# Local window attention: q and k loaded in 512-row blocks, four consecutive rows to a partition

## The chip, the cores and the metric

The kernel runs on one core of one Trainium2 chip. The profile is one execution of the same program taken by the hardware profiler; its span is about 1.8 us shorter than the timed execution it belongs to.

## The reference

Attention inside windows of 64 tokens, with q, k, v of shape (4, 4096, 1536) in float32:

```python
q_w = q.reshape(B, nw, W, D)            # W = 64, nw = S // W; k_w, v_w likewise
logits = np.einsum('bnwd,bnud->bnwu', q_w, k_w) * D ** -0.5
logits = logits - logits.max(axis=-1, keepdims=True)
attn = np.exp(logits)
attn = attn / attn.sum(axis=-1, keepdims=True)
out = np.einsum('bnwu,bnud->bnwd', attn, v_w)
```

Each input and the output is 100.66 MB, so 402.65 MB have to cross HBM whatever the kernel does.

## The kernel before

One group is 128 tokens (two windows). For each of the 128 groups, three loads issued by POOL convert float32 to bf16, PE transposes q and k chunk by chunk, DVE copies the transposed chunks out of PSUM (the memory that PE writes) to SBUF, PE makes the logits, ACT takes the exponential of the two diagonal blocks, PE multiplies by v, ACT scales the result while copying it out of PSUM (the evacuation), and SP stores.

```python
for b in range(B):
    for g in range(n_groups):
        t0 = g * P
        q_nat = q_pool.tile([P, D], bf16)                       # q, k, v pools: 3 buffers each
        nc.gpsimd.dma_start(out=q_nat, in_=q[b, t0:t0 + P, :])
        # ... k_nat and v_nat likewise
        qkt = qkt_pool.tile([P, 2 * n_chunks, 128], bf16)
        for bank in range(3):
            tp = tp_psum.tile([P, 8, 128], bf16)
            # ... 8 PE transposes of q and k chunks into tp
            nc.vector.tensor_copy(out=qkt[:, bank * 8:(bank + 1) * 8, :], in_=tp)
        # ... 12 matmuls into lg
        attn = attn_pool.tile([P, P], bf16)                     # 3 buffers
        nc.gpsimd.memset(attn, 0.0)
        # ... exp of two 64x64 blocks into attn; row sums (matmul with ones); reciprocal
        for cc in range(3):
            # ... av = attn^T v, 512 columns
            nc.scalar.mul(out_sbuf[:, cc * 512:(cc + 1) * 512], av, recip)
        nc.sync.dma_start(out=out[b, t0:t0 + P, :], in_=out_sbuf)
```

The softmax here doesn't subtract the row's maximum and nothing guards it: scores larger than these inputs give would overflow.

Of the kernel before, what the change touches and what calls it, by code (L numbers as in the profile page):

```python
# [1 line left out]

# [5 lines left out]


@with_exitstack
def kernel(
    ctx: ExitStack,
    tc: tile.TileContext,
    q: bass.AP,
    k: bass.AP,
    v: bass.AP,
    out: bass.AP,
):
    nc = tc.nc  # L20
    fp32 = mybir.dt.float32
    bf16 = mybir.dt.bfloat16

    B, S, D = q.shape
    W = 64
    P = 128
    n_groups = S // P
    n_chunks = D // 128
    scale = float(D) ** -0.5

    EXP = mybir.ActivationFunctionType.Exp

    const_pool = ctx.enter_context(tc.tile_pool(name="const_pool", bufs=1))
    q_pool = ctx.enter_context(tc.tile_pool(name="q_pool", bufs=3))
    k_pool = ctx.enter_context(tc.tile_pool(name="k_pool", bufs=3))
    v_pool = ctx.enter_context(tc.tile_pool(name="v_pool", bufs=3))
    qkt_pool = ctx.enter_context(tc.tile_pool(name="qkt_pool", bufs=2))
    attn_pool = ctx.enter_context(tc.tile_pool(name="attn_pool", bufs=3))
    out_pool = ctx.enter_context(tc.tile_pool(name="out_pool", bufs=3))
    small_pool = ctx.enter_context(tc.tile_pool(name="small_pool", bufs=4))  # L40

    tp_psum = ctx.enter_context(tc.tile_pool(name="tp_psum", bufs=3, space=bass.MemoryType.PSUM))
    lg_psum = ctx.enter_context(tc.tile_pool(name="lg_psum", bufs=2, space=bass.MemoryType.PSUM))
    av_psum = ctx.enter_context(tc.tile_pool(name="av_psum", bufs=3, space=bass.MemoryType.PSUM))

    identity = const_pool.tile([128, 128], bf16)
    make_identity(nc, identity)
    ones_col = const_pool.tile([128, 1], bf16)
    nc.gpsimd.memset(ones_col, 1.0)

    for b in range(B):
        for g in range(n_groups):
            t0 = g * P

            q_nat = q_pool.tile([P, D], bf16)
            nc.gpsimd.dma_start(out=q_nat, in_=q[b, t0:t0 + P, :])  # L56
            k_nat = k_pool.tile([P, D], bf16)
            nc.gpsimd.dma_start(out=k_nat, in_=k[b, t0:t0 + P, :])  # L58
            v_nat = v_pool.tile([P, D], bf16)
            nc.gpsimd.dma_start(out=v_nat, in_=v[b, t0:t0 + P, :])  # L60

            qkt = qkt_pool.tile([P, 2 * n_chunks, 128], bf16)
            for bank in range(3):
                tp = tp_psum.tile([P, 8, 128], bf16)
                for j in range(8):
                    slot = bank * 8 + j
                    c, is_k = divmod(slot, 2)
                    src = k_nat if is_k else q_nat
                    nc.tensor.transpose(  # L69
                        tp[:, j, :], src[:, c * 128:(c + 1) * 128], identity  # L70
                    )
                nc.vector.tensor_copy(  # L72
                    out=qkt[:, bank * 8:(bank + 1) * 8, :], in_=tp
                )

            lg = lg_psum.tile([P, 136], fp32)
            for c in range(n_chunks):
                nc.tensor.matmul(  # L78
                    lg[:, 0:128],
                    lhsT=qkt[:, 2 * c + 1, :],  # L80
                    rhs=qkt[:, 2 * c, :],
                    start=(c == 0),
                    stop=(c == n_chunks - 1),
                )

            attn = attn_pool.tile([P, P], bf16)
            nc.gpsimd.memset(attn, 0.0)  # L87
            nc.scalar.activation(  # L88
                out=attn[0:W, 0:W], in_=lg[0:W, 0:W], func=EXP, scale=scale
            )  # L90
            nc.scalar.activation(  # L91
                out=attn[W:P, W:P], in_=lg[W:P, W:P], func=EXP, scale=scale
            )

            nc.tensor.matmul(  # L95
                lg[:, 128:129], lhsT=attn, rhs=ones_col, start=True, stop=True
            )
            recip = small_pool.tile([P, 1], fp32)
            nc.vector.reciprocal(out=recip, in_=lg[:, 128:129])  # L99

            out_sbuf = out_pool.tile([P, D], fp32)
            for cc in range(3):
                av = av_psum.tile([P, 512], fp32)
                nc.tensor.matmul(  # L104
                    av,
                    lhsT=attn,
                    rhs=v_nat[:, cc * 512:(cc + 1) * 512],
                    start=True,
                    stop=True,
                )  # L110
                nc.scalar.mul(out_sbuf[:, cc * 512:(cc + 1) * 512], av, recip)  # L111

            nc.sync.dma_start(out=out[b, t0:t0 + P, :], in_=out_sbuf)


# [1 line left out]
_INS = ['q', 'k', 'v']  # L117
_OUTS = [((4, 4096, 1536), 'float32')]


# [23 lines left out]
```

## Time and profile before

| | before |
|---|---|
| time, median of 13 runs | 974.66 us (973.48 to 976.4) |
| span of the profile | 971.7 us |
| HBM traffic over the span | 414 GB/s |
| the same between 200 and 800 us | 418.9 GB/s |
| from the last load's landing to the end | 8.2 us |

The third row is the page's own figure. The fourth and fifth are worked out from the trace's DMA packet records: every data packet is counted with its larger, float32 side (6144 bytes for one row), and its bytes are spread evenly over its recorded time. All rates called "steady rate" below are made in this way over 200 to 800 us.

Lines of the page of the kernel before: busy time by engine, the span in 40 slices (busy tenths), the DMA queues (packets, MB, share of 16 engines), groups of instructions (busy us, mean ns | idle before them, releaser), and DMA issues (KB each, us to landing).

```profile
span 971.7 us, 13347 instructions
PE 580.6 (60%) x5120; PEld 432.2 (44%) x5120; DVE 277.2 (29%) x512; ACT 292.8 (30%) x641; POOL 230.4 (24%) x519
...
DMA  9999999999999999999999999999999999999997
...
q0 software_dynamic: 55296, 151.02, 79.2%
q1 hardware_dynamic: 18432, 100.67, 26.2%
...
L69 PE MATMUL tp<-identity,q_nat 128*128 128x128 bf16 x1536 | 337.8, 273 | 214.0 <-DMA q_nat<-in_q_dram 214.0
...
L111 ACT ACTIVATE out_sbuf<-av,recip 128x512 f32<-128x512 f32 x384 | 235.8, 685 | 257.6 <-PE av L104 253.1
...
L72 DVE COPY qkt<-tp 128x1024 bf16<-128x1024 bf16 x384 | 255.8, 689 | 142.1 <-PE tp L69 132.3
...
out_dram<-out_sbuf SPq DMA_DIRECT2D x128, 768.0 KB, 7.8
q_nat<-in_q_dram POOLq DMA_DIRECT2D x128, 384.0 KB, 16.3
```

The DMA row is at 9 tenths in all slices but the last, while no compute engine is busy more than 60%. PE, the busiest of them, stands idle for q_nat 214.0 us. The DMA engines bound this kernel. Queue q0 carries the loads; 55296 packets are 49152 data packets (one row each) and 6144 completion packets of 4 bytes, 16 for each of 384 loads. GB/s counts the SBUF side, where a loaded row is bf16, so its value moves with the mix of loads and stores and is not the HBM rate.

### The profile page before, as it was taken

The page shows a single profiled execution, that of the slowest core. Times are in us where ns is not written, and L with a number is a line of the kernel's source. Part 1 is how long each engine was busy: PE and PEld are TensorE (multiplying, and loading weights), DVE is VectorE, ACT ScalarE, POOL GpSimd, SP SyncE. Part 2 cuts the span into 40 slices and gives each one's busy share as a digit, 9 for nine tenths or more (in the row PEclk, how much of TensorE's full clock was granted, in tenths as well). Part 3 has the DMA queues.
Part 4 walks back from the last instruction along what each step waited for, and adds up shares of the span by engine and source line. Part 5 has one row for each costly group of instructions (what it writes and reads, how often), then busy time and mean ns, then how long its engine had stood idle before and what let it go on. Part 6 is the DMA issues. An engine that isn't in the chain of part 4 may idle for free. (4 is left out here: it accounts for less than half of the span.)

```text
span 971.7 us, 13347 instructions
## 1 busy us (share of the span) xinstructions
PE 580.6 (60%) x5120; PEld 432.2 (44%) x5120; DVE 277.2 (29%) x512; ACT 292.8 (30%) x641; POOL 230.4 (24%) x519
## 2 busy tenths in 40 slices
PE   4665765656556566465565655675546656576564
PEld 3444544444444344344444444454434434354443
DVE  2222332223222232232222322223222322232222
ACT  2222322223223232232222322233223222232233
POOL 4222222222122222222222222222222222222220
PEclk9677667678677776776767767657787676766767
DMA  9999999999999999999999999999999999999997
GB/s 184 265 259 269 265 259 260 264 269 259 259 263 261 268 259 259 273 257 263 259 260 274 259 259 261 264 267 259 259 270 261 262 259 259 272 261 259 263 261 230
DMA packets 73791, 252.53 MB, mean 260 GB/s; under 512 B 8192, under 2 KB 8192, under 8 KB 73728
## 3 DMA queue, kind: packets, MB, share of 16 engines
q0 software_dynamic: 55296, 151.02, 79.2%
q1 hardware_dynamic: 18432, 100.67, 26.2%
q8 instruction: 40, 0.66, 0.2%
q14 instruction: 23, 0.19, 0.0%
HBM read 301.99 MB, written 100.66 MB: 414 GB/s over the span
## 5 line engine op out<-in xcount | busy, mean ns | idle before, releaser
L69 PE MATMUL tp<-identity,q_nat 128*128 128x128 bf16 x1536 | 337.8, 273 | 214.0 <-DMA q_nat<-in_q_dram 214.0
L69 PE MATMUL tp<-identity,k_nat 128*128 128x128 bf16 x1536 | 270.8, 277 | 169.7 <-DMA k_nat<-in_k_dram 169.7
L111 ACT ACTIVATE out_sbuf<-av,recip 128x512 f32<-128x512 f32 x384 | 235.8, 685 | 257.6 <-PE av L104 253.1
L69 PEld LDWEIGHTS <-k_nat 128*128 128x128 bf16 x1536 | 190.1, 129 | 253.7 <-DMA k_nat<-in_k_dram 196.8
L69 PEld LDWEIGHTS <-q_nat 128*128 128x128 bf16 x1536 | 192.5, 126 | 241.0 <-DMA q_nat<-in_q_dram 240.3
L72 DVE COPY qkt<-tp 128x1024 bf16<-128x1024 bf16 x384 | 255.8, 689 | 142.1 <-PE tp L69 132.3
L60 POOL DMA_DIRECT2D v_nat<-in_v_dram x128 | 67.7, 529 | 612.4 <-PE tp L69 582.2
L78 PE MATMUL lg<-qkt 128*128 128x128 bf16 x1536 | 178.5, 262 | 1.0 <-DVE qkt L72 0.8
L99 DVE RECIPROCAL recip<-lg 128x1 f32<-128x1 f32 x128 | 21.5, 168 | 546.3 <-PE lg L95 532.0
L104 PE MATMUL av<-v_nat,attn 128*128 128x512 bf16 x384 | 158.2, 541 | 0.0
L88 ACT ACTIVATE attn<-lg 64x64 bf16<-64x64 f32 x128 | 27.8, 217 | 403.2 <-PE lg L78 403.2
L78 PEld LDWEIGHTS <-qkt 128*128 128x128 bf16 x1536 | 134.3, 121 | 9.2 <-DVE qkt L72 9.2
L56 POOL DMA_DIRECT2D q_nat<-in_q_dram x128 | 67.7, 529 | 66.3 <-PE tp L69 60.6
L58 POOL DMA_DIRECT2D k_nat<-in_k_dram x128 | 68.3, 533 | 38.5 <-DMA v_nat<-in_v_dram 32.0
L104 PEld LDWEIGHTS <-attn 128*128 128x128 bf16 x384 | 37.3, 122 | 28.5 <-issue 23.5
L87 POOL MEMSET attn<- 128x128 bf16 x128 | 28.7, 224 | 0.0
L91 ACT ACTIVATE attn<-lg 64x64 bf16<-64x64 f32 x128 | 27.9, 218 | 1.5
L95 PE MATMUL lg<-ones_col,attn 128*128 128x1 bf16 x128 | 25.0, 196 | 0.7 <-ACT attn L91 0.7
L95 PEld LDWEIGHTS <-attn 128*128 128x128 bf16 x128 | 16.9, 132 | 0.8 <-issue 0.8
L88 ACT ACT_TABLE_LOAD x1 | 1.3, 1283 | 12.5 <-PE lg L78 12.5
masks.py:199 POOL TENSOR_SCALAR_AFFINE_SELECT identity<-identity 128x128 bf16<-128x128 bf16 x1 | 0.3, 304 | 0.1
masks.py:197 POOL MEMSET identity<- 128x128 bf16 x1 | 0.2, 204 | 0.3 <-POOLq L128 0.3
(5 smaller groups left out, 0.5 us busy)
## 6 DMA issues: line engine op xcount, KB each, us to landing
out_dram<-out_sbuf SPq DMA_DIRECT2D x128, 768.0 KB, 7.8
q_nat<-in_q_dram POOLq DMA_DIRECT2D x128, 384.0 KB, 16.3
k_nat<-in_k_dram POOLq DMA_DIRECT2D x128, 384.0 KB, 17.8
v_nat<-in_v_dram POOLq DMA_DIRECT2D x128, 384.0 KB, 15.9
```

What stands on the lines that cost most here:

```text
L56: nc.gpsimd.dma_start(out=q_nat, in_=q[b, t0:t0 + P, :])
L58: nc.gpsimd.dma_start(out=k_nat, in_=k[b, t0:t0 + P, :])
L60: nc.gpsimd.dma_start(out=v_nat, in_=v[b, t0:t0 + P, :])
L69: nc.tensor.transpose(tp[:, j, :], src[:, c * 128:(c + 1) * 128], identity)
L72: nc.vector.tensor_copy(out=qkt[:, bank * 8:(bank + 1) * 8, :], in_=tp)
L78: nc.tensor.matmul(lg[:, 0:128], lhsT=qkt[:, 2 * c + 1, :], rhs=qkt[:, 2 * c, :], start=(c == 0), stop=(c == n_chunks - 1),)
L87: nc.gpsimd.memset(attn, 0.0)
L88: nc.scalar.activation(out=attn[0:W, 0:W], in_=lg[0:W, 0:W], func=EXP, scale=scale)
L91: nc.scalar.activation(out=attn[W:P, W:P], in_=lg[W:P, W:P], func=EXP, scale=scale)
L95: nc.tensor.matmul(lg[:, 128:129], lhsT=attn, rhs=ones_col, start=True, stop=True)
L104: nc.tensor.matmul(av, lhsT=attn, rhs=v_nat[:, cc * 512:(cc + 1) * 512], start=True, stop=True,)
L111: nc.scalar.mul(out_sbuf[:, cc * 512:(cc + 1) * 512], av, recip)
```

## The change

The intent is to load q and k in fewer and larger pieces. A block is 512 rows; partition p receives rows 4p to 4p+3, one contiguous run of 24 KB in DRAM. The transposed q and k then come in a permuted order: the copy of k puts it back in token order by a strided output, q stays permuted, and ACT undoes that as it writes attn. The first and the last block are loaded in groups of 128 rows as before. In the last block, ACT and DVE share the evacuation, and each group is stored in two parts. Cut to its core:

```diff
-    for b in range(B):
-        for g in range(n_groups):
-            q_nat = q_pool.tile([P, D], bf16)
-            nc.gpsimd.dma_start(out=q_nat, in_=q[b, t0:t0 + P, :])
+    def load_qk_sg(b, t0, pool, suffix=""):
+        src_q = q[b, t0:t0 + SG, :].rearrange("(p s) d -> p s d", s=NS)   # NS = 4, SG = 512
+        q_sg = pool.tile([P, NS, D], bf16, name="q_sg" + suffix)
+        nc.gpsimd.dma_start(out=q_sg, in_=src_q)
+        # ... k_sg likewise; qk_pool has 2 buffers of each
...
-                nc.vector.tensor_copy(
-                    out=qkt[:, bank * 8:(bank + 1) * 8, :], in_=tp
-                )
+            nc.vector.tensor_copy(out=qq_t[:, c], in_=tp[:, 0])
+            nc.vector.tensor_copy(
+                out=qk_t[:, c].rearrange("p (x j) -> p j x", j=NS), in_=tp[:, 1]
+            )
...
+        for pi in range(NS):
+            # first and last block: loads and transposes of 128 rows, as before (nat_pool, 3 buffers)
+            v_nat = load_v(b, g_t0, v_pool)                                # 6 buffers, 128 rows as before
...
             attn = attn_pool.tile([P, P], bf16)                           # 4 buffers
             nc.gpsimd.memset(attn, 0.0)
...
+            if not is_last:
+                # ... three evacuations by ACT, one store, as before
+            else:
+                nc.scalar.mul(out_sbuf[:, 0:512], av_tiles[0], recip)
+                nc.vector.tensor_scalar_mul(out_sbuf[:, 512:1024], av_tiles[1], recip)
+                store_out(b, g_t0, out_sbuf, 0, 1024)
+                nc.scalar.mul(out_sbuf[:, 1024:1536], av_tiles[2], recip)
+                store_out(b, g_t0, out_sbuf, 1024, 1536)
```

More of the change, by code (lines that the diff above doesn't have):

```diff
@@ L26 @@
     P = 128
-    n_groups = S // P
+    NS = 4
+    NI = W // NS
+    SG = P * NS
+    n_sg = (B * S) // SG
+    sg_per_b = S // SG
     n_chunks = D // 128
@@ L33 @@
     const_pool = ctx.enter_context(tc.tile_pool(name="const_pool", bufs=1))
-    q_pool = ctx.enter_context(tc.tile_pool(name="q_pool", bufs=3))
-    k_pool = ctx.enter_context(tc.tile_pool(name="k_pool", bufs=3))
-    v_pool = ctx.enter_context(tc.tile_pool(name="v_pool", bufs=3))
+    qk_pool = ctx.enter_context(tc.tile_pool(name="qk_pool", bufs=2))
+    v_pool = ctx.enter_context(tc.tile_pool(name="v_pool", bufs=6))
     qkt_pool = ctx.enter_context(tc.tile_pool(name="qkt_pool", bufs=2))
-    attn_pool = ctx.enter_context(tc.tile_pool(name="attn_pool", bufs=3))
-    out_pool = ctx.enter_context(tc.tile_pool(name="out_pool", bufs=3))
-    small_pool = ctx.enter_context(tc.tile_pool(name="small_pool", bufs=4))
+    nat_pool = ctx.enter_context(tc.tile_pool(name="nat_pool", bufs=3))
+    attn_pool = ctx.enter_context(tc.tile_pool(name="attn_pool", bufs=4))
+    out_pool = ctx.enter_context(tc.tile_pool(name="out_pool", bufs=4))
+    small_pool = ctx.enter_context(tc.tile_pool(name="small_pool", bufs=6))
     tp_psum = ctx.enter_context(tc.tile_pool(name="tp_psum", bufs=3, space=bass.MemoryType.PSUM))
@@ L44, with load_v, store_out @@
     av_psum = ctx.enter_context(tc.tile_pool(name="av_psum", bufs=3, space=bass.MemoryType.PSUM))
+    def load_qk_sg(b, t0, pool, suffix=""):
+        src_q = q[b, t0:t0 + SG, :].rearrange("(p s) d -> p s d", s=NS)
+        q_sg = pool.tile([P, NS, D], bf16, name="q_sg" + suffix)
+        nc.gpsimd.dma_start(out=q_sg, in_=src_q)
+        src_k = k[b, t0:t0 + SG, :].rearrange("(p s) d -> p s d", s=NS)
+        k_sg = pool.tile([P, NS, D], bf16, name="k_sg" + suffix)
+        nc.gpsimd.dma_start(out=k_sg, in_=src_k)
+        return q_sg, k_sg
+    def load_v(b, t0, pool, suffix=""):
+        v_nat = pool.tile([P, D], bf16, name="v_nat" + suffix)
+        nc.gpsimd.dma_start(out=v_nat, in_=v[b, t0:t0 + P, :])
+        return v_nat
+    def store_out(b, t0, out_sbuf, col0, col1):
+        nc.sync.dma_start(out=out[b, t0:t0 + P, col0:col1], in_=out_sbuf[:, col0:col1])
     identity = const_pool.tile([128, 128], bf16)
@@ L49 @@
     nc.gpsimd.memset(ones_col, 1.0)
-    for b in range(B):
-        for g in range(n_groups):
-            t0 = g * P
-            q_nat = q_pool.tile([P, D], bf16)
-            nc.gpsimd.dma_start(out=q_nat, in_=q[b, t0:t0 + P, :])
-            k_nat = k_pool.tile([P, D], bf16)
-            nc.gpsimd.dma_start(out=k_nat, in_=k[b, t0:t0 + P, :])
-            v_nat = v_pool.tile([P, D], bf16)
-            nc.gpsimd.dma_start(out=v_nat, in_=v[b, t0:t0 + P, :])
-            qkt = qkt_pool.tile([P, 2 * n_chunks, 128], bf16)
-            for bank in range(3):
-                tp = tp_psum.tile([P, 8, 128], bf16)
-                for j in range(8):
-                    slot = bank * 8 + j
-                    c, is_k = divmod(slot, 2)
-                    src = k_nat if is_k else q_nat
+    for sg in range(n_sg):
+        b, t0 = sg // sg_per_b, (sg % sg_per_b) * SG
+        is_first = sg == 0
+        is_last = sg == n_sg - 1
+        small = is_first or is_last
+        if not small:
+            q_sg, k_sg = load_qk_sg(b, t0, qk_pool)
+        if not small:
+            qq_t = qkt_pool.tile([P, n_chunks, NS, P], bf16, name="qq_t")
+            qk_t = qkt_pool.tile([P, n_chunks, NS * P], bf16, name="qk_t")
+        for c in range(0 if small else n_chunks):
+            tp = tp_psum.tile([P, 2, NS, P], bf16)
+            for t, x_sg in enumerate((q_sg, k_sg)):
+                for j in range(NS):
@@ L69 @@
                     nc.tensor.transpose(
-                        tp[:, j, :], src[:, c * 128:(c + 1) * 128], identity
+                        tp[:, t, j], x_sg[:, j, c * 128:(c + 1) * 128], identity
                     )
-                nc.vector.tensor_copy(
-                    out=qkt[:, bank * 8:(bank + 1) * 8, :], in_=tp
-                )
+            nc.vector.tensor_copy(out=qq_t[:, c], in_=tp[:, 0])
+            nc.vector.tensor_copy(
+                out=qk_t[:, c].rearrange("p (x j) -> p j x", j=NS), in_=tp[:, 1]
+            )
@@ new lines @@
+        for pi in range(NS):
+            g_t0 = t0 + pi * P
+            if small:
+                q_nat = nat_pool.tile([P, D], bf16, name="q_nat")
+                nc.gpsimd.dma_start(out=q_nat, in_=q[b, g_t0:g_t0 + P, :])
+                k_nat = nat_pool.tile([P, D], bf16, name="k_nat")
+                nc.gpsimd.dma_start(out=k_nat, in_=k[b, g_t0:g_t0 + P, :])
+                qkt_g = nat_pool.tile([P, 3, 2, NS, P], bf16, name="qkt_g")
+                for bank in range(3):
+                    tp = tp_psum.tile([P, 2, NS, P], bf16)
+                    for t, x_nat in enumerate((q_nat, k_nat)):
+                        for j in range(NS):
+                            c = 4 * bank + j
+                            nc.tensor.transpose(
+                                tp[:, t, j], x_nat[:, c * 128:(c + 1) * 128], identity
+                            )
+                    nc.vector.tensor_copy(out=qkt_g[:, bank], in_=tp)
+            v_nat = load_v(b, g_t0, v_pool)
@@ L79 @@
                     lg[:, 0:128],
-                    lhsT=qkt[:, 2 * c + 1, :],
-                    rhs=qkt[:, 2 * c, :],
+                    lhsT=qkt_g[:, c // 4, 1, c % 4] if small
+                    else qk_t[:, c, pi * P:(pi + 1) * P],
+                    rhs=qkt_g[:, c // 4, 0, c % 4] if small
+                    else qq_t[:, c, :, 32 * pi:32 * pi + 32],
                     start=(c == 0),
@@ L87 @@
             nc.gpsimd.memset(attn, 0.0)
-            nc.scalar.activation(
-                out=attn[0:W, 0:W], in_=lg[0:W, 0:W], func=EXP, scale=scale
-            )
-            nc.scalar.activation(
-                out=attn[W:P, W:P], in_=lg[W:P, W:P], func=EXP, scale=scale
-            )
+            lg_v = lg[:, 0:128].rearrange("p (j x) -> p j x", j=NS)
+            at_v = attn.rearrange("p (x j) -> p j x", j=NS)
+            for w in range(2):
+                if small:
+                    s = slice(W * w, W * (w + 1))
+                    nc.scalar.activation(
+                        out=attn[s, s], in_=lg[s, s], func=EXP, scale=scale
+                    )
+                    continue
+                nc.scalar.activation(
+                    out=at_v[W * w:W * (w + 1), :, NI * w:NI * (w + 1)],
+                    in_=lg_v[W * w:W * (w + 1), :, NI * w:NI * (w + 1)],
+                    func=EXP, scale=scale,
+                )
             nc.tensor.matmul(
@@ L101 @@
             out_sbuf = out_pool.tile([P, D], fp32)
+            av_tiles = []
             for cc in range(3):
@@ L110 @@
                 )
-                nc.scalar.mul(out_sbuf[:, cc * 512:(cc + 1) * 512], av, recip)
-            nc.sync.dma_start(out=out[b, t0:t0 + P, :], in_=out_sbuf)
+                av_tiles.append(av)
+            if not is_last:
+                for cc in range(3):
+                    nc.scalar.mul(
+                        out_sbuf[:, cc * 512:(cc + 1) * 512], av_tiles[cc], recip
+                    )
+                store_out(b, g_t0, out_sbuf, 0, D)
+            else:
+                nc.scalar.mul(out_sbuf[:, 0:512], av_tiles[0], recip)
+                nc.vector.tensor_scalar_mul(
+                    out_sbuf[:, 512:1024], av_tiles[1], recip
+                )
+                store_out(b, g_t0, out_sbuf, 0, 1024)
+                nc.scalar.mul(out_sbuf[:, 1024:1536], av_tiles[2], recip)
+                store_out(b, g_t0, out_sbuf, 1024, 1536)
 _INS = ['q', 'k', 'v']
```

## The prediction

> **What bounds the kernel now.** The DMA engines. In the page's slices the mean DMA busy share is 9 tenths in every slice but the last, while PE is busy 60%, ACT 30%, DVE 29%. HBM traffic is 302 MB read and 101 MB written, 414 GB/s over the span. Counting each packet by its larger (fp32) side, the trace's packets in 20 us stretches run at 418 to 420 GB/s from 40 us to 940 us; only the ends are worse. In the waits view PE waits for q_nat and k_nat in every group (214 + 170 us).
>
> **What the packets cost.** The ceiling that the Trainium skill states is 435 GB/s ("DMA: Bandwidth & Descriptors", Specifications): 402.65 MB would take 925 us, and the trace is at 96% of it. A load packet (one 6144-byte fp32 row, 3072 bytes in bf16) is recorded as 248 ns, but packets overlap: start-to-start on an engine is 229 ns. The same page ("Why small descriptors are slow") gives about 3 cycles of overhead per packet on 32-byte beats; 192 + 3 beats at 850 MHz are 229.4 ns, so the trace agrees. Per-packet overhead is thus about 3.5 ns, not 22. Beside these run 16 four-byte completion packets per DMA, 21 ns start-to-start on one queue; a balance of a 20 us stretch (85 data and 10.6 completion packets per engine) leaves up to 48 ns for each.
>
> **What the change does.** q and k come in 512-row blocks with four consecutive rows per partition. I expect each partition's four rows to be one contiguous 24 KB run and one packet.
> - Data: 60 block loads x 8 packets per engine, each saving 3 x 3.5 ns: about 5 us.
> - Completions: DMAs per four groups fall from 16 to 10, about 190 completion packets fewer per engine at 21 to 48 ns: 4 to 9 us.
> - Tail: the last group splits its evacuation between ACT and DVE and stores in two parts: about 1 us.
> - DVE: two copies of 512 instead of one of 1024 (689 ns), the k copy with a strided output; I estimate 0.42 + 0.69 us, DVE to about 45%. PE and ACT stay. None of it is on the critical path.
> - Buffers: q and k have two blocks. The next block is issued once an earlier block's attention is done, an estimated 23 us after its landing, of a period near 30 us; 6 to 15 us of queued loads should remain, so the DMA engines do not starve. Stores share the engines packet by packet with 24 KB loads and will land later (now 7.8 us), within four output buffers.
>
> **Prediction.** 974 - 5 - 6 - 1 = about 962 us, range 951 to 972. Faster by over 2%: 0.10; within 2%: 0.84; slower by over 2%: 0.06. Without any overhead on q and k it would save some 17 us, still under 2%.
>
> **What would show it.** DMA stays 9 tenths; q0 packets fall from 55296 to about 30000; load packets of 12288 bytes with a pitch near 907 ns; GB/s over the span rises to about 418; DVE near 430 us.
>
> **What would make it wrong.** Rows not joined into one packet (then about 967). Large packets with much less overhead than the beat count says, or a better HBM pattern (below 951). PE's order placing a whole block's transposes ahead of the previous block's attention, which would hold back the next loads and starve the DMA engines (above 990).

## More of the kernel before

Times are microseconds of device time for one execution; medians are quoted.

POOL issues loads and also clears attn. The waits view of POOL in the kernel before (waiting instruction <- what released it: us in total, times, longest):

```profile
POOL v_nat L60 <- PE tp L69: 582.2, 119, 8.1
POOL q_nat L56 <- PE tp L69: 60.6, 80, 3.4
POOL k_nat L58 <- DMA v_nat<-in_v_dram: 32.0, 36, 1.5
```

I read the first as the back pressure of three buffers.

## The result, and the profile after

| | before | after |
|---|---|---|
| time, median | 974.66 us (13 runs) | 966.93 us (9 runs) |
| ratio | | 0.992, 95% interval 0.9911 to 0.993 |
| span of the profile | 971.7 us | 965.3 us |
| steady rate, 200 to 800 us | 418.9 GB/s | 422.7 GB/s |
| last load's landing to the end | 8.2 us | 9.2 us |

A ratio is the mean time of one kernel's runs over the mean of the other's in the same rounds, so it is not quite the ratio of the medians. The change gains 0.8%: clear of noise, and below 2%.

The lines of the page after that answer to those of before:

```profile
span 965.3 us, 13070 instructions
PE 505.8 (52%) x5120; PEld 362.8 (38%) x5120; DVE 563.1 (58%) x876; ACT 306.7 (32%) x637; POOL 134.6 (14%) x339
...
DMA  9999999999999999999999999999999999999998
...
q0 software_dynamic: 29376, 151.01, 76.2%
q1 hardware_dynamic: 19008, 100.67, 26.3%
...
L92 DVE COPY qk_t<-tp 128x512 bf16<-128x512 bf16 x360 | 460.3, 1279 | 0.0
L91 DVE COPY qq_t<-tp 128x512 bf16<-128x512 bf16 x360 | 155.5, 432 | 329.0 <-PE tp L88 328.7
L88 PE MATMUL tp<-identity,k_sg 128*128 128x128 bf16 x1440 | 165.2, 241 | 273.2 <-DMA k_sg<-in_k_dram 273.2
...
L165 ACT ACTIVATE out_sbuf<-av,recip 128x512 f32<-128x512 f32 x372 | 226.9, 691 | 36.6 <-PE av L154 15.0
...
out_dram<-out_sbuf SPq DMA_DIRECT2D x124, 768.0 KB, 12.6
...
q_sg<-in_q_dram POOLq DMA_DIRECT2D x30, 1536.0 KB, 25.5
```

The DMA row is unchanged: still 9 tenths nearly everywhere. The load queue has 29376 packets, as expected: 18432 of one row, 7680 of 12288 bytes (24 KB of float32, so the four rows were joined), and 3264 completions. The most frequent start-to-start distance near the length of such a packet is 907 ns, as expected. Stores land later, 12.6 us against 7.8. In whole microseconds with the DMA engines full and stores beside loads, stores are half of the bytes in the kernel before (median 0.50), and a fifth where the loads are in 24 KB packets (0.19, changed kernel): as if the engines took one packet of each in turn. One line is far from the prediction: the strided k copy takes 1279 ns, not 690, so DVE is busy 58% and not 45%.

To see where the time was gained, take the bytes moved by a given moment of the changed kernel and ask when the kernel before had moved as many. The difference is the lead (worked out from the packet records of both traces):

```
at, us of the changed kernel    40    100    300    500    700    880    904    920    950    end
lead over before, us           0.1    1.0    3.0    5.1    6.3    8.0    8.1    5.4    5.2    6.4
```

The lead grows steadily through the run, as a higher rate makes it, and then 2.7 us are lost between 904 and 920 us. This loss is called the hole below. The view by stretches shows the loss (us from the span's start, length, busy us and instructions of each engine, granted clock, share of DMA, GB/s) in the changed kernel:

```profile
900.00:906.00 6.00, 0.00 (x0) 0.00 (x0) 0.00 (x0) 0.00 (x0) 0.00 (x0) 0.50 0.99 251
908.00:912.00 4.00, 3.88 (x24) 2.44 (x24) 3.07 (x6) 3.44 (x8) 1.27 (x3) 0.50 0.70 123
912.00:914.00 2.00, 2.00 (x27) 1.72 (x26) 0.22 (x1) 1.69 (x5) 0.93 (x3) 0.75 0.85 128
914.00:920.00 6.00, 4.59 (x55) 3.07 (x53) 6.00 (x11) 4.15 (x8) 2.70 (x7) 1.00 1.02 303
```

From 908 to 914 us the DMA share falls to 0.70 and 0.85. The timeline of POOL tells why (start, us, instruction, [idle before <- releaser]; the first line is the load that took this place one block earlier):

```profile
864.61 0.53 POOL L53 DMA_DIRECT2D q_sg<-in_q_dram  x1 [4.88 <-PE tp L88]
...
888.42 0.53 POOL L56 DMA_DIRECT2D k_sg<-in_k_dram  x1 [0.24 <-issue]
888.94 1.07 POOL L61 DMA_DIRECT2D v_nat<-in_v_dram  x2
889.98 0.56 POOL L100 DMA_DIRECT2D q_nat<-in_q_dram  x1
909.84 0.20 POOL L128 MEMSET attn<- 128x128 bf16 x1 [19.30 <-PE lg L144]
910.28 0.53 POOL L61 DMA_DIRECT2D v_nat<-in_v_dram  x1 [0.24 <-issue]
910.80 0.55 POOL L102 DMA_DIRECT2D k_nat<-in_k_dram  x1
```

POOL had issued the first small load of the last block at 889.98 us, and then stood in its own queue at a memset of attn, which waited 19.30 us for an attention of the block before. Only after that could it issue more loads. And why did that attention come so late? PE's timeline in the same stretch:

```profile
896.97 0.39 PE L88 MATMUL tp<-identity,q_sg 128*128 128x128 bf16 x4
906.74 0.50 PE L88 MATMUL tp<-identity,k_sg 128*128 128x128 bf16 x3 [9.39 <-DMA k_sg<-in_k_dram]
...
908.22 0.16 PE L144 MATMUL lg<-ones_col,attn 128*128 128x1 bf16 x1
908.24 1.44 PE L154 MATMUL av<-v_nat,attn 128*128 128x512 bf16 x3
```

In PE's order of instructions in this trace, the first transposes of the next block (L88) and two matmuls of the logits (L117) stand before the row sums (L144) and the product with v (L154) of the block before. The transposes of k waited 9.39 us until that k had landed, and nothing behind them ran meanwhile. So the memset, and the loads behind it, waited for a load to land that was itself one of the last in the queue. One block earlier a 512-row load (the q_sg at 864.61 us) and two loads of 128 rows stand in the queue behind the k that PE waits for, and no hole follows; here there are three loads of 128 rows, and they do not cover the wait.

### The profile page after: what moved, and what is told of

It is laid out like the page before. It is cut to its first block, busy times and chain, and to the rows that moved or that the text cites. A ratio compares the mean times of both kernels' runs of the same rounds, so it can differ in the third digit from the quotient of the medians.

```text
span 965.3 us, 13070 instructions
## 1 busy us (share of the span) xinstructions
PE 505.8 (52%) x5120; PEld 362.8 (38%) x5120; DVE 563.1 (58%) x876; ACT 306.7 (32%) x637; POOL 134.6 (14%) x339
## 2 busy tenths in 40 slices
DMA packets 48445, 252.51 MB, mean 262 GB/s; under 512 B 5376, under 2 KB 5376, under 8 KB 40704
## 3 DMA queue, kind: packets, MB, share of 16 engines
q0 software_dynamic: 29376, 151.01, 76.2%
## 5 line engine op out<-in xcount | busy, mean ns | idle before, releaser
L92 DVE COPY qk_t<-tp 128x512 bf16<-128x512 bf16 x360 | 460.3, 1279 | 0.0
L91 DVE COPY qq_t<-tp 128x512 bf16<-128x512 bf16 x360 | 155.5, 432 | 329.0 <-PE tp L88 328.7
L88 PE MATMUL tp<-identity,k_sg 128*128 128x128 bf16 x1440 | 165.2, 241 | 273.2 <-DMA k_sg<-in_k_dram 273.2
L88 PEld LDWEIGHTS <-k_sg 128*128 128x128 bf16 x1440 | 112.2, 109 | 288.5 <-DMA k_sg<-in_k_dram 279.9
L88 PE MATMUL tp<-identity,q_sg 128*128 128x128 bf16 x1440 | 168.6, 243 | 98.8 <-DVE qk_t L92 84.1
L117 PE MATMUL lg<-qq_t,qk_t 128*128 128x128 bf16 x1440 | 174.0, 250 | 38.0 <-DVE qk_t L92 38.0
L88 PEld LDWEIGHTS <-q_sg 128*128 128x128 bf16 x1440 | 105.3, 109 | 153.2 <-DVE qk_t L92 118.8
L154 PE MATMUL av<-v_nat,attn 128*128 128x512 bf16 x384 | 151.7, 460 | 10.4 <-ACT out_sbuf L165 10.3
L117 PEld LDWEIGHTS <-qk_t 128*128 128x128 bf16 x1440 | 119.8, 114 | 73.5 <-DVE qk_t L92 51.3
L154 PEld LDWEIGHTS <-attn 128*128 128x128 bf16 x384 | 36.7, 109 | 13.3 <-issue 9.3
L144 PEld LDWEIGHTS <-attn 128*128 128x128 bf16 x128 | 14.4, 112 | 37.2 <-issue 36.5
L144 PE MATMUL lg<-ones_col,attn 128*128 128x1 bf16 x128 | 22.5, 176 | 9.4 <-ACT attn L138 4.5
L109 PE MATMUL tp<-identity,q_nat 128*128 128x128 bf16 x96 | 12.5, 275 | 13.3 <-DMA q_nat<-in_q_dram 13.3
L109 PE MATMUL tp<-identity,k_nat 128*128 128x128 bf16 x96 | 12.0, 277 | 10.6 <-DMA k_nat<-in_k_dram 10.6
## 6 DMA issues: line engine op xcount, KB each, us to landing
out_dram<-out_sbuf SPq DMA_DIRECT2D x124, 768.0 KB, 12.6
```

The source lines that it names most:

```text
L88: nc.tensor.transpose(tp[:, t, j], x_sg[:, j, c * 128:(c + 1) * 128], identity)
L91: nc.vector.tensor_copy(out=qq_t[:, c], in_=tp[:, 0])
L92: nc.vector.tensor_copy(out=qk_t[:, c].rearrange("p (x j) -> p j x", j=NS), in_=tp[:, 1])
L109: nc.tensor.transpose(tp[:, t, j], x_nat[:, c * 128:(c + 1) * 128], identity)
L117: nc.tensor.matmul(lg[:, 0:128], lhsT=qkt_g[:, c // 4, 1, c % 4] if small else qk_t[:, c, pi * P:(pi + 1) * P], rhs=qkt_g[:, c // 4, 0, c ...
L144: nc.tensor.matmul(lg[:, 128:129], lhsT=attn, rhs=ones_col, start=True, stop=True)
```

## The experiments

There were twelve runs in three batches of four, each batch on one chip together with the kernel before. The batches ran on three chips, so runs are compared by their ratios rather than their medians. The kernels marked so give wrong results; all others were correct. The theories were these. A: the gain is about 5 us from larger data packets and 4 to 9 us from fewer completions, as predicted. B: data packets give all of it. C: completions give all of it.

### Small packets, few DMAs

```diff
-        src_q = q[b, t0:t0 + SG, :].rearrange("(p s) d -> p s d", s=NS)
+        src_q = q[b, t0:t0 + SG, :].rearrange("(s p) d -> p s d", s=NS)      # k likewise; result wrong
```

> The changed kernel with block rows strided, so a block load has 6 KB (fp32) packets and still one DMA; q and k rows are permuted, so its result is wrong on purpose. Theory A (the prediction): 5 us of the gain are data packets, 4 to 9 us completions: this keeps the completions part, about 971 to 972 us. Rival B (data packets give all of it, about 9 us, completions nothing): about 975 us, steady rate back to 419 GB/s. Rival C (completions give all): 967 us.

Measured: 974.6 us, ratio 0.9987 (0.9974 to 1.0001). The order of instructions, as far as the trace has them, is the same on every engine as in the changed kernel, and so is the number of loads; only the packets are smaller. The page's load queue:

```profile
q0 software_dynamic: 52416, 151.01, 79.1%
```

The gain is gone. The steady rate is 419.1 GB/s, and the lead over the kernel before is 0.5 us at 880 us, where the changed kernel had 8.0. The packets are thus worth 7.5 us of lead. The hole at the end is there as well (lead 0.5 us at 904, -1.3 at 920). This is theory B on the whole: fewer completions alone bought half a microsecond in the profiles, and the ratio does not tell the run from the kernel before.

### Large packets, many DMAs

```diff
-        nc.gpsimd.dma_start(out=q_sg, in_=src_q)
+        for i in range(NS):                                                   # k likewise
+            nc.gpsimd.dma_start(out=q_sg[32 * i:32 * i + 32], in_=src_q[32 * i:32 * i + 32])
```

> The changed kernel with each block load cut into four DMAs of 32 partitions: 24 KB packets as in the changed kernel, 16 DMAs per four groups as before. A: loses the completions part, 971 to 975 us. B: unchanged, about 967 us. C: about 975 us.

Measured: 969.69 us, ratio 0.9942 (0.9929 to 0.9954). The time lies between what A and B expected. The steady rate is 421.4 GB/s, between the two. From 100 to 880 us the lead grows by 4.6 us, against 7.0 in the changed kernel, so beside large packets the fewer DMAs are worth 2.3 us there, if the different order (below) has no part in it. The run also loses 3 us before 100 us; that was not pursued. It has no hole at the end; the compiled order of POOL's queue came out differently. The order on the other engines differs too, so this cell is less clean than the one before.

Sorting whole microseconds from 60 to 900 us by what was in flight gives a cleaner view. In stretches with loads alone and the engines full, the mean rates are:

```
loads alone, GB/s            16 loads per 512 rows       10 or fewer per 512 rows
6 KB packets                 421.5 (before)              425.6 (small packets, few DMAs; nearly all such stretches)
24 KB packets                428.0 (large, many DMAs)    431.8 (the changed kernel)
stretches with stores beside 6 KB loads: before 416.9, small-and-few 413.1, changed kernel 412.9
```

Both parts help where loads run alone: about 4 GB/s for fewer completions and 6 for larger packets, and they add. But with stores beside 6 KB loads the rate is lower in both kernels with few DMAs than before. From 60 to 900 us more packets of these two take over 30 ns longer than usual: their excess sums to 3.6 us per engine in small-and-few, 2.2 in the changed kernel, 0.9 before. In these two runs that is where much of the completions' gain is given back. But few DMAs do not force it. A second count of the same kind (whole microseconds with a store, no 24 KB packet and a DMA share of at least 0.97) gives 417.5 before, 413.4 in the changed kernel, 414.0 in this run with as many DMAs as before, and 418.0 and 419.1 in two later runs with few DMAs (ten v buffers; v in blocks). The excess goes the same way: 2.3 us in this run, 0.7 in those two. What stretched those packets and lowered this rate was not found.

### Small packets, many DMAs

```diff
-        nc.gpsimd.dma_start(out=q_sg, in_=src_q)
+        for i in range(NS):                                                   # k likewise
+            nc.gpsimd.dma_start(out=q_sg[:, i], in_=src_q[:, i])
```

> The changed kernel with each block load cut into four DMAs of one row per partition: 6 KB packets and 16 DMAs per four groups, both as before; the compute order of the change stays. A, B and C alike: the steady rate is that of before, 419 GB/s, and the time is before's plus the 2 us lost near the end, 974 to 978 us. If it stays near 967 us, neither packets nor completions explain the gain.

Measured: 1029.95 us, ratio 1.0561 (1.0546 to 1.0575). It was meant as a control and missed by 55 us. Its steady rate is 391.8 GB/s. The waits of POOL and one of the holes:

```profile
POOL attn L130 <- PE lg L146: 349.9, 52, 12.4
POOL q_sg L54 <- DMA q_sg<-in_q_dram: 94.2, 27, 4.5
POOL v_nat L63 <- DMA q_sg<-in_q_dram: 79.8, 32, 4.9
POOL v_nat L63 <- DMA v_nat<-in_v_dram: 75.8, 26, 4.4
```

```profile
450.00:458.00 8.00, 3.77 (x24) 2.48 (x26) 1.22 (x3) 1.87 (x6) 0.00 (x0) 0.50 1.08 212
460.00:462.00 2.00, 1.82 (x28) 1.52 (x27) 1.20 (x2) 1.95 (x5) 1.26 (x3) 1.00 0.84 102
```

From 450 to 458 us the engines are full, and just after it the share falls to 0.84; such a hole stands in every block. POOL waits 94.2, 79.8 and 75.8 us until an earlier load has landed, and then again at the memsets. Counting loads issued by POOL but not landed, by the times in the trace, the most is exactly 8 in all fourteen kernels. The traces also tell where the 8 comes from: the loads raise eight semaphores in turn when they land (100 to 107 in every kernel), and 375 of the 384 loads of this kernel wait for the semaphore of the load eight before them. The compiled program sets this limit; whether the chip has one was not reached. In this kernel one block's q, k and v are 12 loads, so eight of them are less than a block; in the changed kernel a block is six loads. My reading is that small loads cannot put enough bytes in flight to cover the time that POOL stands at the memsets. But the order of the instructions differs here too, and the large-packet run with as many loads has no such holes, so the number of loads is not the whole cause. As a control for packets the run is lost: it tells only that its extra time stands in the holes, and the rate where loads run alone and the engines are full, 424 GB/s from 448 to 458 us, ahead of that hole, is near that of small packets above.

### Eight attn buffers

```diff
-    attn_pool = ctx.enter_context(tc.tile_pool(name="attn_pool", bufs=4))
+    attn_pool = ctx.enter_context(tc.tile_pool(name="attn_pool", bufs=8))
```

> The changed kernel with 8 attn buffers in place of 4, so that the POOL queue's memsets no longer hold the last block's loads behind block 30's attention. If that wait makes the hole of 906 to 914 us in the DMA stream: the hole goes, 2 to 3 us gained, about 964 us, steady rate unchanged. If the hole has another cause: 967 us.

Measured: 966.41 us, ratio 0.9911 (0.9897 to 0.9924), not told apart from the changed kernel. The hole stayed: POOL's timeline shows the next obstacle in its queue at almost the same moment.

```profile
888.68 0.54 POOL L100 DMA_DIRECT2D q_nat<-in_q_dram  x1
909.93 0.53 POOL L61 DMA_DIRECT2D v_nat<-in_v_dram  x1 [20.72 <-PE lg L144]
910.45 0.54 POOL L102 DMA_DIRECT2D k_nat<-in_k_dram  x1
```

### The tail stored at once

```diff
-            if not is_last:
+            if True:
```

> The changed kernel with the last block's evacuation and store as everywhere else: three ACT evacuations, one store per group. The prediction gave the split tail 1 us of gain: then 968 us, and the stretch from the last load's landing to the end is 10 us. Rival: the two smaller stores (4 KB and 2 KB packets, one more DMA) cost as much as the earlier start gains: 966 to 967 us, and the tail stays at 8 to 9 us.

Measured: 967.85 us, ratio 0.9926 (0.9913 to 0.9938). From the last load's landing to the end it takes 10.6 us, against 9.2 in the changed kernel. In the two profiles the split is worth 1.4 us, near the 1 us predicted, although the times alone do not tell the two kernels apart. The prediction did not see that the end of the new order is itself longer: even with the split it is 1 us longer than before.

### The k copy without its stride

```diff
-                out=qk_t[:, c].rearrange("p (x j) -> p j x", j=NS), in_=tp[:, 1]
+                out=qk_t[:, c].rearrange("p (j x) -> p j x", j=NS), in_=tp[:, 1]     # result wrong
```

> The changed kernel with the k copy written without the stride of four (k rows permuted, result wrong on purpose). The copy should fall from 1279 ns to about 430 ns, DVE busy from 563 to about 260 us. If DVE is off the critical path, as predicted: 965 to 967 us, steady DMA rate as in the changed kernel (422.7 GB/s). If the strided copy slows the loads by its length: 3 us or more faster; the hole at 906 us may also shrink, since the last block's attention comes earlier.

Measured: 964.51 us, ratio 0.9894 (0.988 to 0.9907). The copy takes 414 ns. The steady rate is 421.8 GB/s, not higher than in the changed kernel, so the strided copy does not slow the loads in the middle. The 2.4 us between the two medians come at the end: the rate from 900 to 940 us is 419.2 GB/s, against 390.3, and the lead of 6.8 us at 904 is still 6.6 at 920. This looked like proof that the long copy made the hole. The strided read below speaks against it. This is the one run that beats the changed kernel beyond noise (its interval ends at 0.9907, the changed kernel's begins at 0.9911).

### Eight attn and ten v buffers

```diff
-    v_pool = ctx.enter_context(tc.tile_pool(name="v_pool", bufs=6))
-    attn_pool = ctx.enter_context(tc.tile_pool(name="attn_pool", bufs=4))
+    v_pool = ctx.enter_context(tc.tile_pool(name="v_pool", bufs=10))
+    attn_pool = ctx.enter_context(tc.tile_pool(name="attn_pool", bufs=8))
```

> The changed kernel with 8 attn and 10 v buffers. With 8 attn buffers alone the hole stayed, because the queue then stopped at the next v load, which waited for a v buffer until 910 us. If buffers alone make the hole: it goes now, 2 to 3 us gained over the changed kernel, about 964 us. If not, the loads wait for something else as well.

Measured: 967.87 us, ratio 0.9925 (0.9913 to 0.9938). The hole is gone, in a compiled order that differs in part from the changed kernel's, as it does with eight attn buffers alone: 416.6 GB/s from 900 to 940 us, and the lead is 8.6 us at 904 and 8.8 at 950. The last load lands at 954.3 us, 1.8 us sooner than in the changed kernel. Yet the span ends at 966.1 us, for the end after that landing has grown from 9.2 to 11.8 us. The last load that POOL issues, in the changed kernel and then in this one, tells why:

```profile
934.95 0.53 POOL L61 DMA_DIRECT2D v_nat<-in_v_dram  x1 [0.25 <-issue]
...
931.07 0.53 POOL L102 DMA_DIRECT2D k_nat<-in_k_dram  x1 [1.32 <-ACT out_sbuf L165]
```

In the changed kernel a v comes last; here it is a k, whose transposes, logits and exponential stand before the product with v. By the semaphores' times the last k lands at 953.8 us in the changed kernel and at 954.6 us here, and in both the span ends 11.5 us after it. The loads were through sooner, but the one that the end waits for came later.

### v in blocks as well

```diff
+            v_sg = vb_pool.tile([P, NS, D], bf16, name="v_sg")                # 3 buffers
+            nc.gpsimd.dma_start(out=v_sg, in_=v[b, t0:t0 + SG, :].rearrange("(s p) d -> p s d", p=P))
...
-            v_nat = load_v(b, g_t0, v_pool)
+            v_nat = load_v(b, g_t0, v_pool) if small else v_sg[:, pi]         # also 8 attn buffers, one store at the end
```

> A version meant to beat both: the changed kernel with v too loaded in blocks of 512 rows by one DMA (6 KB packets, three fewer completions per four groups), 8 attn buffers, and one store per group at the end. In load-only stretches the completions removed from q and k were worth about 1% of the rate (421.5 to 425.6 GB/s); v's are a third of the loads, so I expect 1 to 3 us from them and up to 2 us from the hole: 962 to 966 us. If completions do not matter beside stores: 967 us.

Measured: 968.32 us, ratio 0.993 (0.9917 to 0.9944). The steady rate is the highest here, 423.3 GB/s, and the lead is 9.6 us at 920. The end takes 12.9 us after the last landing, again that of a k, and gives it all back.

### A strided read in place of the strided write

```diff
-                out=qk_t[:, c].rearrange("p (x j) -> p j x", j=NS), in_=tp[:, 1]
+                out=qk_t[:, c].rearrange("p (x j) -> p x j", j=NS),
+                in_=tp[:, 1].rearrange("p j x -> p x j"),
```

> The changed kernel with the stride of the k copy moved from its SBUF output to its PSUM input; the result stays right. If the 1279 ns come from the strided write: about 690 ns, as the prediction estimated for the copy, the hole near 906 us shrinks or goes, 964 to 966 us. If any stride in the copy costs that much: still about 1280 ns and 967 us.

Measured: 967.47 us, ratio 0.9922 (0.9908 to 0.9935), correct. The copies of this run:

```profile
L91 DVE COPY qq_t<-tp 128x512 bf16<-128x512 bf16 x360 | 148.5, 412 | 494.2 <-PE tp L88 493.9
L92 DVE COPY qk_t<-tp 128x512 bf16<-128x512 bf16 x360 | 243.8, 677 | 0.0
```

The same elements in the same places take 677 ns instead of 1279: the stride costs that much only on the output side. But the time did not move, and the hole is there (387.8 GB/s from 900 to 940 us). POOL's queue has the order of the changed kernel:

```profile
890.43 0.56 POOL L101 DMA_DIRECT2D q_nat<-in_q_dram  x1
910.53 0.20 POOL L129 MEMSET attn<- 128x128 bf16 x1 [19.55 <-PE lg L145]
910.98 0.54 POOL L61 DMA_DIRECT2D v_nat<-in_v_dram  x1 [0.24 <-issue]
```

On every engine the order of instructions in the trace is that of the changed kernel. So a copy of about half the length, in the same order, leaves the hole as it was. The plain copy had changed more than the length: the instructions were also put in another order. PE's timeline of the run with the plain copy, to be held against the one of the changed kernel above:

```profile
900.40 0.50 PE L88 MATMUL tp<-identity,q_sg 128*128 128x128 bf16 x3 [13.85 <-DMA q_sg<-in_q_dram]
...
901.87 0.16 PE L144 MATMUL lg<-ones_col,attn 128*128 128x1 bf16 x1
901.90 0.59 PE L154 MATMUL av<-v_nat,attn 128*128 128x512 bf16 x1
...
908.04 0.23 PE L88 MATMUL tp<-identity,k_sg 128*128 128x128 bf16 x1 [1.61 <-DMA k_sg<-in_k_dram]
```

Here PE waited for q_sg, and the attention of the block before (901.87 us) ran 6 us before k_sg had landed (908.04 us). The memset was released at 903.49 us, with the 512-row load of k still under way, and the next loads were issued in time. What decides, on this reading, is which transposes stand ahead of the attention in PE's order. This is read from the two traces; no run changed that order alone.

### The k copy on ACT

```diff
-            nc.vector.tensor_copy(
+            nc.scalar.copy(
                 out=qk_t[:, c].rearrange("p (x j) -> p j x", j=NS), in_=tp[:, 1]
             )
```

> The changed kernel with the k copy issued on ACT, which is 32% busy; the result stays right. If only the length of the DVE burst per block makes the hole: an ACT copy of 0.6 to 0.8 us beside DVE's 0.43 us halves the burst, the hole goes as with the plain copy, 964 to 965 us. If ACT's evacuations are held up by the copies: stores later, 967 us or more.

Measured: 968.16 us, ratio 0.9928 (0.9915 to 0.994). ACT is no faster at this copy, 1419 ns, and is now busy 74%. A hole appears later, near 936 us, and the end takes 11.7 us.

### Two attempts at a faster kernel

Both join v blocks to one of the two last edits (with 4 attn buffers and the split tail of the changed kernel).

```diff
-            nc.vector.tensor_copy(
+            nc.scalar.copy(                                                   # strided output, as above
-            v_nat = load_v(b, g_t0, v_pool)
+            v_nat = load_v(b, g_t0, v_pool) if small else v_sg[:, pi]
```

> A version meant to beat both kernels: the k copy on ACT and v in blocks of 512 rows. v blocks alone raised the steady rate from 422.7 to 423.4 GB/s but lost it in the last 20 us, where compute came late. With the shorter burst the end should not be late: 962 to 964 us. If the end is lost again: 966 us.

Measured: 967.05 us, ratio 0.992 (0.9907 to 0.9934).

```diff
-                out=qk_t[:, c].rearrange("p (x j) -> p j x", j=NS), in_=tp[:, 1]
+                out=qk_t[:, c].rearrange("p (x j) -> p x j", j=NS),
+                in_=tp[:, 1].rearrange("p j x -> p x j"),
-            v_nat = load_v(b, g_t0, v_pool)
+            v_nat = load_v(b, g_t0, v_pool) if small else v_sg[:, pi]
```

> The same with the strided read on DVE in place of the copy on ACT: 962 to 965 us if the strided read is about 690 ns; 968 us, as v blocks alone, if the read is as slow as the write.

Measured: 968.96 us, ratio 0.9938 (0.9926 to 0.9951). Both have no hole and both end late, 11.4 and 11.8 us after the last landing. None of the correct variants beats the changed kernel beyond noise. A version with the strided read and the plain copy's order on PE was not tried; the plain copy's 964.5 us is an estimate of what it could reach. The late ends show one pattern in all fourteen traces: the span ends 10.9 to 11.7 us after the last k lands (12.1 in the two runs with small packets, 12.5 in the two with one store at the end). In the kernel with ten v buffers, the three runs with v in blocks and the one with the copy on ACT, that k is the last load of all; in the others a v lands 2 to 3 us after it. The plain copy's last k lands at 951.0 us, 2.8 us sooner than in the changed kernel, which is about its gain. This is read from the traces; no run swapped those two loads alone.

## Why the prediction was right or wrong

The time was inside the range, 966.93 us against 962 and a range of 951 to 972, and the verdict, within 2%, was right. Point by point:

- **The bound.** Right. The DMA row stays at 9 tenths, and the halved or doubled work of DVE (281 us busy in the plain copy, 563 in the changed kernel) leaves the steady rate alone. The ceiling argument held too: loads alone in 24 KB packets ran at 431.8 GB/s in the changed kernel and 432.8 in the plain copy, the highest means seen, below the 435 that the Trainium skill states ("DMA: Bandwidth & Descriptors", Specifications). The page gives that figure for the SBUF side of the fabric; applying it to the larger, float32 side of each packet was the prediction's step, and these rates agree with it.
- **Data packets, 5 us.** The mechanism was right and the size somewhat low: the estimate of 3.5 ns per packet gave 5 us, and the runs show 7.5 us of lead between the changed kernel and the same with small packets. The measured pitches leave 9 ns for every four rows joined (4 x 229 - 907), 4.3 us for the 480 such packets of an engine. Another 1.4 us is the difference in stretched packets (3.6 against 2.2 us per engine), and the rest was not traced.
- **Completions, 4 to 9 us.** This is the term that was mis-sized. The step that failed is "a balance of a 20 us stretch (85 data and 10.6 completion packets per engine) leaves up to 48 ns for each". That balance gave all time not explained by a 229 ns pitch to completions, but before, stretches with stores run at 416.9 GB/s and with loads alone at 421.5, so part of that time goes with the stores. The runs show 0.5 us from fewer completions alone and 2.3 us beside large packets. Their number fell by 176 per engine (8192 to 5376 over 16 engines), near the 190 forecast, so it is the worth of each that was off. Why the gain of loads alone is lost beside stores in these runs stays open.
- **The tail, 1 us gained, "no starving".** The split is worth 1.4 us in the profiles, but the end of the block-wise order is longer, 9.2 us against 8.2. The prediction looked at the buffers of the steady state, where the queued loads indeed sufficed (no microsecond from 60 to 900 us has a DMA share under 0.9), and not at the change from a large block to a small one. There the loads ran out and 2.7 us were lost. The prediction named the mechanism among what would make it wrong, PE's order placing transposes ahead of the previous block's attention, but as a loss in every block. The wait is there in nearly every block (PE waited for k_sg 29 times, 273.2 us in all), and it left a hole only once.
- **DVE, 0.69 us for the k copy.** Wrong by almost two: 1279 ns. The estimate was right for a strided read (677 ns), and the copy's stride is on the write. It cost no time here that a run could show.
- The sum: about 8 us of lead at 880 us where some 11 were predicted, less what the end lost, gives 6.4 us in the profile and 7.7 in the medians. That the total came within 5 us of the forecast is partly luck: the packets gave 2.5 us more than predicted, the completions at least 1.7 less, and the end lost time instead of gaining it.

The Trainium skill's "Perfetto Trace Analysis" (What "DMA-bound" means) says that for a kernel bound on DMA engines large descriptors are what matter. This case agrees, with a size: 6 KB to 24 KB packets on nearly half of the traffic gave 0.7% (ratio 0.992 against 0.9987).

## What to carry to other kernels

When the DMA engines are already at 96% of their ceiling, work out first what all overhead together can give; here an estimate of 17 us, of which somewhat under half was got. Of the two ways to coarsen a load, larger contiguous packets paid more than fewer DMAs, and only an experiment with the one and without the other could show it. The hole in this stream was a matter of which loads are queued ahead of an instruction that waits for compute, and it stood where the block size changes. Closing it gained nothing where the load that the last computation needs first, here a k, then landed no sooner.

## What the Trainium skill lacked or had wrong

- "VectorE: DVE Perf Modes" (Mode 1x (REGULAR), the baseline) lists odd strides among what its one-result-per-cycle mode takes, and that section names no cost for a stride. A bf16 copy of 128x512 from PSUM with an output step of four elements took 1279 ns; with the step moved to the input (there of 128 elements), 677 ns; with none, 412 to 432 ns. The 677 fit an estimate from the page (512 results at its 0.96 GHz are 533 ns, the rest taken as a fixed part), the 1279 do not. ACT took 1419 ns for the same strided output.
- "DMA: Bandwidth & Descriptors" (Why small descriptors are slow) agrees with the pitches of 229 and 907 ns, but it says nothing of stores beside loads: 421.5 GB/s with loads alone and 416.9 with stores, at the same packet size.
- No page read has a limit on loads in flight from POOL, and these runs show none of the chip: there were at most 8 in all fourteen traces, but the program itself waits on eight semaphores in turn for them.
